# A two-block transformer on one Trainium2 core: new order in the opening and around two projections, other products in retention

## The chip, the cores and the metric

The kernel runs on one core of one Trainium2 (trn2) chip. The metric is device time in microseconds of one execution; lower is better. The core's engines are TensorE (PE; its weight loads are PEld), VectorE (DVE), ScalarE (ACT), GpSimd (POOL) and SyncE (SP), which issues the DMAs. [...]

## The reference

The input `x` is 256 tokens of width 1024, in float32. Two blocks follow one another.

The first block: `h = rms_norm(x)`, a projection `h @ w_in` gives q, k, v of four attention branches (stick-breaking, dilated, forgetting, differential) and a gate; `x += sum(sigmoid(gate) * (branch @ w_branch)) @ w_out`; then `x += square(relu(rms_norm(x) @ w_up)) @ w_down`, and a last `rms_norm(x)`.

The second block has a retention layer and a sparse-attention layer, each followed by a SwiGLU layer, all with a norm in front and behind. In retention q and k are rotated in pairs, the scores are multiplied by a decay, the outputs are normed per head, multiplied by `silu(g)` and projected back with `w_ro`:

```
q, k = rotate_pairs(q, cos, sin), rotate_pairs(k, cos, sin) / 16
o = (q @ k.T * decay) @ v                      # four heads, v is 512 wide
o = o * rsqrt(mean(o * o) + eps) * silu(g)
x = x + rms_norm(o @ w_out)
```

The sparse-attention layer projects shared keys and values and queries, and a small gate matrix (`w_ng`, 48 columns), and projects back with `w_no`.

## The kernel before, in words

Tokens lie in two row tiles (t = 0, 1) of 128. All large products are done at near float32 accuracy from two parts: every operand is split into a high part `hi` (fp32r) and a low part `lo = x - hi`, and three products hi·hi, hi·lo, lo·hi are summed (`mm3`, L246 to L251). A weight comes in halves of 128 x 1024 (or 128 x 772 for the first): `each_half` (L225) issues the DMA into one of four `raw` buffers, ScalarE makes `whi` (L234), VectorE `wlo` (L237); six such pairs can be held (`wsp`), more where a pool is added. This is called a split below.

`Inputs.a(t)` norms the rows t: two square sums (ScalarE L406, VectorE L411), their mean (L414), the power -0.5 on GpSimd (L416), the scaling `xn` (L193, L194). `Inputs.b(t)` transposes `xn` on TensorE (L436) and makes the eight column pairs of hi (ScalarE L209) and lo (VectorE L210).

`an_groups` (L297) starts each layer: two groups of four weight halves. All halves that can be held are multiplied for one row tile first; ahead of the last of them stands `inp.b(1)`, so the second rows' norm is needed only there; then the second row tile follows. `project_back` (L357) ends each layer: the products of all chunks but the last three go into four banks (two row tiles, two halves of the columns) at once; the last six halves are held and used row tile by row tile: for t = 0 all held halves into bank 0 and then all into bank 1, `residual(0)` and `nxt.a(0)` follow, then t = 1, where `nxt.b(0)` stands before the last half.

Two forms of a projection with the weight as the stationary operand: `ws_chunk` (L343) does three products of 256 columns per 128 rows of the weight, `ws_wide` (L259) one of 512 columns (hi and lo of x side by side, L274) and one of 256 (L276), and adds the two halves of the bank on ScalarE (L277) and VectorE (L278).

In the opening (L499 to L505) SyncE issues the first rows, two small constants, the second rows and then weights. TensorE does 12 products of zeros (`warm_up`). `run` writes `inp.a(0)`, the second rows' DMA, `inp.b(0)`, `inp.a(1)` in this order, then `mix`.

The mlp's `residual` (L1065) adds the rows (L449), norms them, applies the final gain (L1070), and is followed by the norm for retention. In retention, `rotated` (L1124) multiplies the projection's bank with cosine and sine (L1127, L1129) and adds on GpSimd (L1130); `scores` uses the result in full float32; `outputs` (L1158) multiplies the weights `at` with v in full float32 (L1164, L1166). In `nsa` the small matrix `wng` is split before the layer's `an_groups`.

The order of the instructions on each engine is set when the program is built. A planner of the framework takes them from the order of the code, and places one earlier when it expects its inputs earlier; engines run their lists in that order. `tc.issue_after(i)` adds an edge: what is written inside it is placed behind `i` on `i`'s engine. `behind(engine)` (L471) does so with the engine's last instruction so far.

## Time and profile before

| | |
|---|---|
| median of the runs shown (1204.67 to 1211.26) | 1204.8 us |
| the profiled execution | 1208.24 us |
| its span, first to last instruction | 1206.5 us |
| TensorE busy, share of the span | 98% |
| VectorE, ScalarE, GpSimd | 67%, 55%, 7% |
| HBM, over the span | 173 GB/s |

All rows come from the one profiled execution. Times in a view are microseconds from the span's start. In a timeline row stand start, duration, engine, line, operation, output<-inputs, shape, and in brackets the idle time of the engine before it with what ended it. [...]

### The profile page before, as it was taken

How to read it: one execution, taken by the hardware profiler on the slowest of the kernel's cores; microseconds unless marked ns; L12 is line 12 of the kernel's file. 1: busy time of each engine (PE TensorE's matmuls, PEld its weight loads, DVE VectorE, ACT ScalarE, POOL GpSimd, SP SyncE). 2: the span in 40 equal slices, each digit the busy share in tenths (PEclk: the TensorE clock that was granted, in tenths of full speed). 3: DMA queues.
4: the chain of work that ended last, by engine and by line, in shares of the span. 5: the costliest groups of instructions: out<-in, count | busy, mean ns of one | idle time of the engine just before them, and what ended most of it. 6: DMA issues, size and time to landing. Idle time of an engine off the chain costs nothing.

```text
span 1206.5 us, 18129 instructions
## 1 busy us (share of the span) xinstructions
PE 1184.8 (98%) x6848; PEld 1014.4 (84%) x6848; DVE 806.3 (67%) x1413; ACT 662.9 (55%) x1148; POOL 80.8 (7%) x87
## 2 busy tenths in 40 slices
PE   8999999999999998999999999999999999999997
PEld 6999889887888887899878888888889877888886
DVE  7757877667746667557456665657778967655663
ACT  5545765655644454543555554556567876645561
POOL 1000001200000000012000000000100530000000
PEclk8999999999999999999999999999999999999999
DMA  7654454536455565554546355556655226555560
GB/s 239 196 175 158 140 191 158 175 126 230 161 192 187 191 208 181 177 194 158 166 148 213 120 192 189 192 185 212 209 194 179 72 70 205 179 189 186 189 205 35
DMA packets 60775, 210.11 MB, mean 174 GB/s; under 512 B 7120, under 2 KB 9808, under 8 KB 60560
## 3 DMA queue, kind: packets, MB, share of 16 engines
q1 hardware_dynamic: 60688, 208.95, 53.0%
q8 instruction: 54, 0.88, 0.3%
q14 instruction: 33, 0.27, 0.1%
HBM read 207.84 MB, written 1.08 MB: 173 GB/s over the span
## 4 chain that ended last, share of the span: by engine, by line
PE 82%; DVE 7%; DMA 5%; ACT 3%; issue 1%; POOL 0%; SPq 0%; DVEq 0%; POOLq 0%; ACTq 0%
PE b L274 19%; PE b L249 15%; PE b L251 15%; PE b L250 15%; PE b L276 9%; DVE wlo L237 3%; ACT whi L234 1%; PE b L436 1%; DMA raw<-w_up 1%; DMA raw<-w_no 1%; DMA raw<-w_rv 1%; PE b L1536 1%; DMA raw<-w_ck 1%; DMA wng<-w_ng 1%; ACT s L1503 1%
## 5 line engine op out<-in xcount | busy, mean ns | idle before, releaser
L237 DVE TENSOR_TENSOR wlo<-raw,whi 128x1024 fp32r<-128x1024 f32 (+3 forms) x432 | 470.9, 1103 | 265.1 <-ACT whi L234 262.2
L234 ACT ACTIVATE whi<-raw 128x1024 fp32r<-128x1024 f32 (+1 forms) x384 | 401.6, 1050 | 383.6 <-issue 116.5
L274 PE MATMUL b<-x,whi 128*128 128x512 f32 x1024 | 362.7, 398 | 0.0
L276 PE MATMUL b<-x,wlo 128*128 128x256 f32 x1024 | 286.3, 280 | 0.0
L249 PE MATMUL b<-whi,x 128*128 128x512 f32 (+1 forms) x720 | 283.9, 395 | 1.8 <-ACT x L209 1.0
L250 PE MATMUL b<-wlo,x 128*128 128x512 f32 (+1 forms) x720 | 280.7, 390 | 1.0 <-DVE wlo L237 0.8
L251 PE MATMUL b<-whi,x 128*128 128x512 f32 (+1 forms) x720 | 279.8, 390 | 0.6 <-DVE x L210 0.6
L274 PEld LDWEIGHTS b<-x,whi 128*128 128x128 f32 x1024 | 192.2, 188 | 45.9 <-issue 0.3
L276 PEld LDWEIGHTS b<-x,wlo 128*128 128x128 f32 x1024 | 193.1, 189 | 0.9
L249 PEld LDWEIGHTS b<-whi,x 128*128 128x128 f32 x720 | 136.1, 189 | 34.5 <-ACT x L209 4.3
L251 PEld LDWEIGHTS b<-whi,x 128*128 128x128 f32 x720 | 136.3, 189 | 29.9 <-DVE x L210 1.3
L250 PEld LDWEIGHTS b<-wlo,x 128*128 128x128 f32 x720 | 136.4, 189 | 28.7 <-DVE wlo L237 1.9
L249 PE MATMUL b<-x,whi 128*128 128x256 f32 x480 | 137.6, 287 | 0.0
L251 PE MATMUL b<-x,wlo 128*128 128x256 f32 x480 | 135.5, 282 | 0.4 <-DVE wlo L237 0.4
L250 PE MATMUL b<-x,whi 128*128 128x256 f32 x480 | 135.4, 282 | 0.0
L249 PEld LDWEIGHTS b<-x,whi 128*128 128x128 f32 x480 | 91.5, 191 | 2.1 <-issue 1.5
L251 PEld LDWEIGHTS b<-x,wlo 128*128 128x128 f32 x480 | 91.5, 191 | 0.6 <-DVE wlo L237 0.6
L250 PEld LDWEIGHTS b<-x,whi 128*128 128x128 f32 x480 | 91.6, 191 | 0.1
L416 POOL TENSOR_TENSOR rstd<-ms,mhalf 128x1 f32<-128x1 f32 x22 | 13.8, 626 | 686.5 <-DVE ms L414 686.5
L210 DVE SCALAR_TENSOR_TENSOR x<-b,gc,x 128x128 fp32r<-128x128 f32 x112 | 36.7, 348 | 20.2 <-ACT x L209 18.3
L209 ACT ACTIVATE x<-b,gc 128x128 fp32r<-128x128 f32 x112 | 37.9, 367 | 21.7 <-PE b L436 16.5
L1503 ACT ACTIVATE s<-s,nm 128x128 f32<-128x128 f32 (+1 forms) x64 | 28.2, 444 | 2.6 <-DVE rz L1507 1.4
(277 smaller groups left out, 1014.8 us busy)
## 6 DMA issues: line engine op xcount, KB each, us to landing
raw<-w_fi SPq DMA_DIRECT2D x88, 512.0 KB, 4.5
raw<-w_fo SPq DMA_DIRECT2D x44, 512.0 KB, 4.5
raw<-w_gate SPq DMA_DIRECT2D x32, 512.0 KB, 4.2
raw<-w_up SPq DMA_DIRECT2D x32, 512.0 KB, 3.9
raw<-w_down SPq DMA_DIRECT2D x32, 512.0 KB, 3.9
raw<-w_qk SPq DMA_DIRECT2D x24, 512.0 KB, 4.1
raw<-w_rv SPq DMA_DIRECT2D x16, 512.0 KB, 4.8
raw<-w_rqk SPq DMA_DIRECT2D x16, 512.0 KB, 4.5
```

What stands on the lines that cost most here:

```text
L209: k.nc.scalar.activation(hi, ps[:, j, :], AF.Copy, scale=g)
L210: k.nc.vector.scalar_tensor_tensor(lo, ps[:, j, :], g, hi.bitcast(F32), op0=OP.mult, op1=OP.subtract)
L234: nc.scalar.activation(hi[:, :n], r, AF.Copy)
L237: nc.vector.tensor_tensor(lo[:, c], r[:, c], hi[:, c].bitcast(F32), op=OP.subtract)
L249: mm(out, lhs[0], rhs[0], start=start, stop=False)
L250: mm(out, lhs[0], rhs[1], start=False, stop=False)
L251: mm(out, lhs[1], rhs[0], start=False, stop=stop)
L274: mm(ps.rearrange("p a t -> p (a t)"), half[0][:, s], x[2][:, k].rearrange("p a t -> p (a t)"), start=k == 0, stop=False)
L276: mm(ps[:, 0], half[1][:, s], x[0][:, k, :], start=False, stop=k == KT - 1)
L416: nc.gpsimd.tensor_tensor(r, ms, self.mhalf[:, :1], op=OP.pow)
L436: self.nc.tensor.transpose(ps[:, j, :], src[:, j * 128:(j + 1) * 128], self.ident)
L1503: nc.scalar.activation(s[:, a, i, :], s[:, a, i, :], AF.Exp, bias=nm[:, a, i:i + 1], scale=-1.0, accum_out=z[:, a, i:i + 1])
```

## The change

Seven edits:

- Opening: the second rows' DMA goes behind the DMAs of two weight halves; the splits are queued behind the first rows' scaling (`rows_done`), the second rows' norm behind the first rows' column pairs (`columns_done`).
- Two sets of 12 products that nobody reads (`keep_warm`, 256 columns, bf16), behind the first rows' transposes and behind the first half's products.
- The GpSimd biases of the differential branch are queued behind the second rows' norm.
- `project_back`, where it has four chunks (w_out, w_no): for t = 0 the held halves go into bank 0 and bank 1 alternately, one half apart. In the others the order stays.
- Entry of retention: the splits of w_rv from the third half on are queued behind the add of the first rows' residual in the mlp.
- Retention: q and k use `ws_wide`, and the scores of a head come one chunk later; the outputs use `mm3` on split operands instead of float32 products.
- Sparse attention: the split of `wng` is written and queued behind the layer's first products.

```
-    def an_groups(self, groups, n, inp, order=(0, 1), extra=0):
+    def an_groups(self, groups, n, inp, order=(0, 1), extra=0, then=None):
...
                 for j in range(4):
+                    queued = self.queued(self.rows_done if len(hs) > 1 or then else ())
...
-                    hs.append((i, 2 * j, next(chunk)))
+                    with queued:
+                        hs.append((i, 2 * j, next(chunk)))
+                    if then and len(hs) == 2:
+                        then()
...
                 mul(j, order[0])
+                if then and j == 0:
+                    self.keep_warm()
...
         accs = [[self.bank() for _ in range(2)] for _ in range(2)]
+        self.rows_done = ()
...
+            lead = min(len(held), 1 if nk == KT else len(held))
             for t in range(2):
-                for banks in ((0,), (1,)) if t == 0 or not nxt else ((0, 1),):
-                    for a in held[:-1]:
-                        self.as_t(accs[t], *a, t, banks)
-                    if t and nxt:
+                if t == 0 or not nxt:
+                    order = [(i, 0) for i in range(lead)]
+                    for i in range(len(held)):
+                        order += [(i + lead, 0)] * (i + lead < len(held)) + [(i, 1)]
+                else:
+                    order = [(i, n) for i in range(len(held)) for n in range(2)]
+                for i, n in order:
+                    if t and nxt and (i, n) == (len(held) - 1, 0):
                         nxt.b(0)
-                    self.as_t(accs[t], *held[-1], t, banks)
+                    self.as_t(accs[t], *held[i], t, (n,))
...
+    def keep_warm(self):
+        w = self.ident.bitcast(BF)
+        ps = self.bank()[:, :256]
+        with self.behind(self.nc.tensor):
+            for _ in range(WARM):
+                self.nc.tensor.matmul(ps, w[:, :128], w, start=True, stop=True)
+    def lasts(self):
+        order = list(reversed(self.nc.cur_bb.bb.instructions))
+        return [next(i for i in order if i.engine == e.engine) for e in (self.nc.scalar, self.nc.vector)]
+    def queued(self, instructions):
+        es = ExitStack()
+        for i in instructions:
+            es.enter_context(self.tc.issue_after(i))
+        return es
...
             inp.a(0)
-            nc.sync.dma_start(self.x[:, 1, :], self.I["x"][:, 1, :])
+            self.rows_done = self.lasts()
             inp.b(0)
-            inp.a(1)
+            self.keep_warm()
+            columns_done = self.lasts()
+            def second_rows():
+                nc.sync.dma_start(self.x[:, 1, :], self.I["x"][:, 1, :])
+                with self.queued(columns_done):
+                    inp.a(1)
+                self.second_norm = [i for i in nc.cur_bb.bb.instructions if i.engine == nc.gpsimd.engine][-1:]
...
-                nc.gpsimd.tensor_scalar(b, mk[:, kind, :], -slope, None, op0=OP.mult)
+                with self.queued(self.second_norm):
+                    nc.gpsimd.tensor_scalar(b, mk[:, kind, :], -slope, None, op0=OP.mult)
...
-            vs = self.an_groups([("w_v", 0), ("w_v", 1)], NB, inp)
+            vs = self.an_groups([("w_v", 0), ("w_v", 1)], NB, inp, then=second_rows)
...
             def residual(t, acc):
                 self.add_residual(t, acc)
+                if t == 0:
+                    self.rows_done = self.lasts()
...
-            def rotated(s, ps):
-                a = tp.tile([128, 2, T], F32, tag=f"rot{s}", name="rot")
+            def rotated(s, i):
+                a = self.ws_wide("w_rqk", i, xin, tp.tile([128, 2, T], F32, tag=f"rot{s}", name="rot"))
                 b = tp.tile([128, 2, T], F32, tag="rotb", name="rotb")
-                nc.vector.tensor_tensor(a, ps, cs, op=OP.mult)
                 for j in range(2):
-                    nc.vector.tensor_tensor(b[:, j, :], ps[:, 1 - j, :], sn[:, j, :], op=OP.mult)
+                    nc.vector.tensor_tensor(b[:, j, :], a[:, 1 - j, :], sn[:, j, :], op=OP.mult)
+                nc.vector.tensor_tensor(a, a, cs, op=OP.mult)
                 nc.gpsimd.tensor_tensor(a, a, b, op=OP.add)
...
-                    if s == 0 and qk:
+                    if s == 1 and qk:
                         scores(h - 1, *qk)
...
+                    steps += 1
+                    if steps == 2 and g == 0:
+                        scores(3, *qk)
+                    if steps == (3 if g == 0 else 1):
+                        src = [v[:, t, g * 512:(g + 1) * 512] for t in range(2)] + [at[:, g, :]]
+                        for tag, x in zip(("rot0", "rot1", "rotb"), src):
+                            hl = [tp.tile([128, 2, T], F32, tag=tag, name=tag).rearrange("p a t -> p (a t)").bitcast(F32R)
+                                  [:, :x.shape[1]] for _ in range(2)]
+                            self.split(*hl, x)
+                            parts.append(hl)
...
-                    mm(p, at[:, g, t * 128:t * 128 + 128], v[:, 0, vs], start=True, stop=t == 0)
+                    self.mm3(p, [x[:, t * 128:t * 128 + 128] for x in w], v0, True, t == 0)
                     if t:
-                        mm(p, at[:, g, T:384], v[:, 1, vs], start=False, stop=True)
+                        self.mm3(p, [x[:, T:384] for x in w], v1, False, True)
...
-            wg = tp.tile([128, KT, 96], F32R, name="wg")
-            self.split(wg[:, :, :48], wg[:, :, 48:], raw.rearrange("p (k c) -> p k c", k=KT))
...
                 nc.scalar.activation(vn[:, t, :], ps[1][t], AF.Copy)
+            wg = tp.tile([128, KT, 96], F32R, name="wg")
+            with self.queued(self.lasts()):
+                self.split(wg[:, :, :48], wg[:, :, 48:], raw.rearrange("p (k c) -> p k c", k=KT))
```

## Rows read from the trace of the kernel before

**Rows 1.** The page's busy times and its line of granted clock, 40 slices.
```profile
PE 1184.8 (98%) x6848; PEld 1014.4 (84%) x6848; DVE 806.3 (67%) x1413; ACT 662.9 (55%) x1148; POOL 80.8 (7%) x87
...
PEclk8999999999999999999999999999999999999999
```

**Rows 2.** Timeline of the opening: start, duration, instruction, idle time before it.
```profile
5.83 0.54 POOL L416 TENSOR_TENSOR rstd<-ms,mhalf 128x1 f32<-128x1 f32 x1 [4.75 <-DVE ms L414]
9.13 0.69 DVE L411 CUSTOM_DVE_ANT_0 junk<-res 128x512 bf16<-128x512 f32 x1 [3.44 <-DMA res<-x]
...
10.12 0.85 ACT L234 ACTIVATE whi<-raw 128x772 fp32r<-128x772 f32 x1 [0.18 <-DMA raw<-w_v]
...
10.63 2.12 PE L436 MATMUL b<-cm,xn 128*128 128x128 f32 x8 [4.55 <-DVE xn L193]
...
11.79 0.37 ACT L209 ACTIVATE x<-b,gc 128x128 fp32r<-128x128 f32 x1 [0.20 <-PE b L436]
...
21.11 0.42 PE L249 MATMUL b<-whi,x 128*128 128x386 f32 x1
```

**Rows 3.** Stretches: from:to, length, busy per engine, granted clock, DMA share, GB/s.
```profile
10.60:15.70 5.10, 5.07 (x17) 3.94 (x17) 3.82 (x11) 4.87 (x12) 0.38 (x1) 0.50 0.51 161
...
476.60:480.00 3.40, 2.72 (x11) 2.56 (x12) 1.17 (x4) 1.71 (x4) 0.02 (x1) 0.50 0.00 0
...
998.80:1002.20 3.40, 3.40 (x9) 2.62 (x9) 2.26 (x3) 1.49 (x2) 0.00 (x0) 0.50 0.81 252
...
543.00:555.80 12.80, 12.80 (x106) 12.70 (x105) 8.74 (x11) 4.24 (x4) 3.50 (x2) 1.00 0.50 164
```

**Rows 4.** Timeline of TensorE at the ends of w_out and w_no.
```profile
277.78 0.74 PE L249 MATMUL b<-whi,mx 128*128 128x512 f32 x2 [0.75 <-ACT whi L234]
...
995.80 0.47 PE L249 MATMUL b<-whi,x 128*128 128x512 f32 x1
997.04 0.50 PE L250 MATMUL b<-wlo,x 128*128 128x512 f32 x1 [0.76 <-DVE wlo L237]
...
998.56 1.03 PE L249 MATMUL b<-whi,x 128*128 128x512 f32 x2 [0.79 <-ACT whi L234]
```

**Rows 5.** Timeline at the entry of retention.
```profile
469.98 1.29 DVE L237 TENSOR_TENSOR wlo<-raw,whi 128x512 fp32r<-128x512 f32 x2 [2.81 <-ACT whi L234]
...
471.19 0.68 DVE L449 TENSOR_TENSOR res<-res,b 128x512 f32<-128x512 f32 x1
...
477.28 1.94 PE L436 MATMUL b<-cm,xn 128*128 128x128 f32 x8 [3.34 <-DVE xn L193]
```

**Rows 6.** Timeline of TensorE: L249 in w_rqk, 30 apart, and L274 in w_up, 34 apart.
```profile
544.65 0.28 PE L249 MATMUL b<-x,whi 128*128 128x256 f32 x1
...
555.45 0.28 PE L249 MATMUL b<-x,whi 128*128 128x256 f32 x1
...
440.34 0.40 PE L274 MATMUL b<-x,whi 128*128 128x512 f32 x1
...
452.35 0.40 PE L274 MATMUL b<-x,whi 128*128 128x512 f32 x1
```

**Rows 7.** Chain that ended last, around a retention output: start, us, what.
```profile
586.53 0.23 PE b L251
...
588.07 1.72 PE b L1164 x4
```

**Rows 8.** Groups of VectorE instructions: count, busy us, mean ns, idle before.
```profile
L237 DVE TENSOR_TENSOR wlo<-raw,whi 128x1024 fp32r<-128x1024 f32 x328 | 402.6, 1233 | 243.9 <-ACT whi L234 241.1 <-PE b L251 0.6 <-issue 0.4
...
L278 DVE TENSOR_TENSOR up<-b,up 128x256 f32<-128x256 f32 x36 | 15.1, 421 | 15.5 <-ACT up L277 15.5
...
L243 DVE TENSOR_TENSOR x<-sg,x 128x512 fp32r<-128x512 f32 x18 | 12.3, 685 | 0.7 <-ACT x L242 0.7
```

**Rows 9.** Timeline at the entry of sparse attention.
```profile
877.60 0.52 ACT L242 ACTIVATE wg<-wng 128x384 fp32r<-128x384 f32 x1 [0.78 <-DMA wng<-w_ng]
...
878.69 0.50 PE L249 MATMUL b<-whi,x 128*128 128x512 f32 x1 [0.48 <-ACT x L209]
```

**Rows 10.** Timeline of VectorE in the rotation, beside a GpSimd add from 544.62.
```profile
544.97 2.02 DVE L237 TENSOR_TENSOR wlo<-raw,whi 128x1024 fp32r<-128x1024 f32 x1
```

More of the change, by code (lines that the diff above doesn't have):

```diff
@@ L489, in run @@
             self.ps = self.pool(es, "ps", 8, bass.MemoryType.PSUM)
+            self.rows_done = ()
             nc.scalar.preload_act_table_set("natural_log_exp_and_others")
@@ L502, in run @@
             inp.a(0)
-            nc.sync.dma_start(self.x[:, 1, :], self.I["x"][:, 1, :])
+            self.rows_done = self.lasts()
             inp.b(0)
-            inp.a(1)
+            self.keep_warm()
[5 more added lines that the diff above has]
+                self.second_norm = [i for i in nc.cur_bb.bb.instructions if i.engine == nc.gpsimd.engine][-1:]
             with ExitStack() as e1:
                 qkp = self.pool(e1, "b1qk", 5)
-                mx = self.mix(inp, cm, qkp)
+                mx = self.mix(inp, cm, qkp, second_rows)
                 inp = Inputs(self, ("mlp_norm_g",))
@@ L517, in run, with mix @@
             self.ffn(inp, 1, None)
-    def mix(self, inp, cm, qkp):
+    def mix(self, inp, cm, qkp, second_rows):
         nc, I = self.nc, self.I
@@ L1144, in retention @@
                 for s in range(2):
-                    rot.append(rotated(s, self.ws_chunk("w_rqk", 2 * h + s, xin)))
-                    if s == 0 and qk:
+                    rot.append(rotated(s, 2 * h + s))
+                    if s == 1 and qk:
                         scores(h - 1, *qk)
@@ L1152, in gates, with outputs @@
                 sg = tp.tile([128, 2, 512], F32, tag="sg", name="sg", bufs=1)
+                parts, steps = [], 0
                 for _ in self.an_steps("w_rg", g, 512, xin,
                                        lambda t, ps: nc.scalar.activation(sg[:, t, :], ps, AF.Silu)):
-                    pass
-                return sg
-            def outputs(g, sg):
-                vs = slice(g * 512, (g + 1) * 512)
+                    steps += 1
[8 more added lines that the diff above has]
+                            parts.append(hl)
+                return sg, parts
+            def outputs(g, sg, parts):
+                v0, v1, w = parts
                 ss = self.st.tile([128, 2], F32, tag="ss2", name="ss2")
@@ L1186, in retention @@
                 sg = gates(g)
-                if g == 0:
-                    scores(3, *qk)
-                else:
+                if g:
                     transposed(yn)
-                yn = outputs(g, sg)
+                yn = outputs(g, *sg)
             e1.close()
```

## Prediction

> **What bounds the kernel now.** The page's first part comes first: TensorE is busy for 1184.8 of 1206.5 us, VectorE for 806.3, ScalarE for 662.9 [rows 1]. So TensorE sets the end, and there are two things to look for: products that could be cheaper, and the few places where it waits. The granted-clock line of the page shows the second kind: every slice is at 9 but the first, at 8. I then read the timeline where TensorE's rows show idle time, and the stretches of half clock. Four places matter.
>
> The opening. The norm factor of the first 128 rows leaves GpSimd at 5.83+0.54 us, but VectorE's next instruction is the square sum of the second rows, which waits 3.44 us for their DMA and starts at 9.13; only then comes the first rows' scaling, and with it TensorE's first transposes (10.63, after 4.55 us without a product) [rows 2]. [...]
>
> The two 8-row projections (w_out, w_no), where TensorE waits for the last weight halves [rows 4]; the entry of retention, where it waits 3.34 us for the normalised rows and then works at 0.50 [rows 3, 5]; and a small wait in the sparse-attention entry.
>
> Against what the numbers hold: the span is 1206.5, the execution 1208.24, 1.7 around it; the median of the runs shown is 1204.8. I take terms from the trace and subtract them from the median. A difference of 1%, 12 us, is about what a measurement of this kernel can tell from no change.
>
> **The change part by part.**
>
> *Opening.* The second rows' DMA goes behind two weight halves, their norm behind the first rows' eight column pairs, and every weight split behind the first rows' scaling. So the scaling can follow GpSimd at 6.4 us, and the transposes start half a microsecond behind it, near 7.0 instead of 10.63: 3.6 us earlier. The half clock of 10.6 to 15.7 costs 5.1 × 0.5 = 2.55 us [rows 3]; with warm-up products until 6.08 (10.63 less the idle 4.55), transposes from 7.0 and 12 filler products behind them, TensorE is hardly idle, so I expect the clock to stay up. Together 6.15 us at most. What is late next: the weight splits. TensorE runs six halves for the first rows before it needs the second rows; before, the product behind the second rows' transposes starts at 21.11 [rows 2]. Until then ScalarE must do eight column copies of 0.37, six splits of 0.85 and one norm of about 1.5, in all 9.6 us, and VectorE about as much; from 7.0 that ends near 17 to 18, not at 15. So I take 3.0 of the 6.15. The two sets of filler products are 24 × 256 columns; 256 columns take 0.12 us at full clock (a third of a triple [rows 6]), so 2.9 us, beside waits for weights; if that cover is gone they cost 2.9. The second rows' norm is the added wait: queued behind it on ScalarE and VectorE are the later splits, and TensorE's transposes of the second rows wait for it; its scaling ends some 4 us behind the eighth column, near 15, needed at 17. The GpSimd biases behind it are products of the mask for a branch that comes much later: nothing. SyncE's queue issues the second rows' DMA two places later, and the two weights one place earlier. Bounds: -2 (fillers bare, second rows late by a little) to 6.
>
> *w_out and w_no.* For the first rows, the held halves are now used for bank 0 and bank 1 alternately, so a half that is late is wanted later. The number of products is the same. w_out: a wait of 0.75 for the last half [rows 4]; a bank is three products of 0.23 us [rows 7], and four banks more pass before that half is wanted, 2.8 us, against 0.75: gone, 0.9 with the restart. w_no: waits of 0.76 and 0.79, which with the start-up of the products around them are 2.0 us, and the clock at 0.50 from 998.8 to 1002.2, worth 1.7 [rows 3, 4]. The last half's high part lets its product go at 998.56, its low part, one VectorE split of 1.23 later [rows 8], comes near 999.8. The old order would have asked for that half at 996.5 (the bank before it begins at 995.80), the new one asks four banks later, at 999.3, so 0.5 remains: 2.0 + 1.7 - 0.5 = 3.2. The norm of the first rows starts that much earlier, its chain is as long as before. Bounds: 0 to 4.6 for both; I take 0.9 and 3.2.
>
> *Entry of retention.* The w_rv splits from the third half on are queued behind the first rows' residual. Before, VectorE waits 2.81 us for the seventh half's split, does it at 469.98, and only then adds the residual (471.19), whose bank had been ready near 467 (30 products of 0.23 before the last one at 473.9) [rows 5, 7]. Two norms follow, and TensorE gets its transposes at 477.28, 3.34 us late. Without that wait the chain starts 4 us earlier and the transposes are ready when TensorE arrives. Lost there: the 3.34 us, and half of the 2.7 us from 477.28 to 480.0 in which the clock is 0.50: 4.7 in all [rows 3, 5]. What is late next: VectorE. Splits of halves three to seven (5 × 1.29) used to run before 471, in gaps; now they run between 467 and 485, with two norm chains (an estimate of 4.0 each, five passes over 512 columns at 0.69 [rows 8] and small ones), eight column copies of 0.35 and 1.4 for the second residual: from 473.3 about 13.7 us for the 12 us to the need of the seventh half. So 1.5 comes back as waiting: 3.2. The four weight buffers behind the waiting splits stay full meanwhile, so SyncE's queue stands; the halves it would fetch are wanted after 485 only. Bounds: -4 (all five splits, 6.5 us, ahead of the first chain, and the clock falls again) to 4.7.
>
> *Rotation of q and k.* Eight chunks go from three products of 256 columns to one of 512 and one of 256. Three take (555.45 - 544.65) / 30 = 0.360 us, the pair (452.35 - 440.34) / 34 = 0.353 [rows 6]; 8 × 16 × 0.0068 = 0.9 us. [...] Each chunk adds two ScalarE copies and two VectorE adds of 0.42 [rows 8], and the scores of a head now come one chunk later. VectorE is busy for 8.74 us of a 12.8 us stretch of two chunks [rows 3]; 1.7 more still fits: hidden.
>
> *Retention outputs.* Six full-precision passes per head, 0.43 us each (1.72 for four [rows 7]), become nine of 0.23: 2.58 - 2.07 = 0.51, four heads 2.05 us. For that, three splits per head: ScalarE 1.7, VectorE 1.9 us (0.69 for 512 columns [rows 8]) beside the 11 us of a gate projection. Hidden; bare it would cost 4 × 1.9 = 7.7.
>
> *Sparse-attention entry.* ScalarE waits for a small weight's DMA until 877.60, and the column copy queued behind that split holds TensorE for 0.48 [rows 9]; the split moves behind the projections, where the first use is 17 us away: 0.5.
>
> **Sum.** 3.0 (opening) + 0.9 + 3.2 (w_out, w_no) + 3.2 (retention entry) + 0.9 + 2.05 (rotation, outputs) + 0.5 = 13.75 us. 1204.8 - 13.75 = 1191.05; for the profiled execution it would be 1194.5.
>
> **The rivals.**
>
> *Handed back (1197).* The openings of both kinds are bound by splits: TensorE arrives earlier and waits for VectorE. For it: at both places I found VectorE's work within 10% of the time there is. Then opening and retention entry give 2 together instead of 6.2, and the clock falls once more in one of them (1.7): 13.75 - 4.2 - 1.7 = 7.85. Against it: both begin with a wait that has nothing to do with load.
>
> *Both entries pay in full (1187).* If the splits fit into the gaps and the clock never falls, the opening gives 6 and the retention entry 4.7: 18.25 us. For it: VectorE and ScalarE are at 67% and 55% over the span [rows 1]; against it the work counted above for these places.
>
> *VectorE becomes the bound in retention (1212, slower).* Place: rotation and gates. Price: the added VectorE work all on the path, 8 × 0.84 + 4 × 1.9 = 14.4 us; GpSimd's eight adds at up to 0.8 each, 6.4. A VectorE split beside a GpSimd add took 2.02 us where such a split takes 1.23 on average [rows 8, 10]. Then 1204.8 - 13.75 + 20.8 = 1212; if each of the eight waits also brings a stretch at 0.50 (1.7 each, as in w_no), 1225. It decides at the point where VectorE needs more than TensorE's 12.4 us for two chunks; from 8.74 + 1.7 = 10.4 it lacks 2. [...]
>
> *The ordering edges do nothing (1198).* If the planner's order was not what made VectorE wait, only w_out, w_no, rotation and outputs pay: 7.05. Against it: the rows show the instruction that waits, and what stands behind it.
>
> **How the numbers follow.** Forecast 0.50 (1186 to 1195, its middle below the 1% line at 1192.8); handed back 0.22; both in full 0.13; edges do nothing 0.08; VectorE bound 0.07. Faster by over 1%: 0.13 + 0.38 of the forecast's half + 0.02 = 0.53. Slower by over 1% needs the last rival with the clock: 0.05. Within 1%: 0.42. The range, 1184 to 1200, holds the forecast, the first rival and most of the second and fourth.
>
> **What would show it.** Right: first transposes near 7 us and no stretch at 0.50 after 6 us; the product behind the second rows' transposes near 18; L449 of the first rows before the third w_rv split, and no TensorE gap over 1 us in front of the transposes; no wait over 0.6 us in w_out and w_no, no half clock at w_no; outputs as rows of 0.23. Wrong: half clock in the opening all the same; a gap of over 2 us at the entry of retention, filled on VectorE by splits; TensorE rows in the rotation that wait for VectorE; fillers with a weight's products ready behind them.

## The result, and the profile after

| | before | after |
|---|---|---|
| median (runs) | 1206.07 us (4) | 1196.4 us (4) |
| lowest to highest | 1204.67 to 1211.26 | 1194.91 to 1197.22 |
| ratio, 95% interval | | 0.9917 [0.9898, 0.9936] |
| profiled execution, its span | 1208.24, 1206.5 | 1197.22, 1195.4 |

The kernel is 0.83% faster, 9.7 us between the medians and 11.0 between the profiled executions, inside the range 1184 to 1200; I had forecast 13.75. (The 1204.8 from which I subtracted was the median of the first three of the four runs before; with the fourth it is 1206.07.)

Where it came from is read from TensorE's rows: I take the start of the same instruction in both traces at seven marks, and the differences of the stretches add up to that of the spans (the start of a layer is its "entry", which ends at the transposes of the second rows). The numbers in brackets are the marks, before and after.

| TensorE's stretch | before | after | gain | forecast |
|---|---|---|---|---|
| opening: start to the product behind the second rows' transposes | 21.11 | 19.76 | 1.35 | 3.0 |
| to the mlp's first transposes (288.92, 286.94) | 267.81 | 267.18 | 0.63 | 0.9, with the next |
| to the mlp's second transposes (302.45, 299.90) | 13.53 | 12.96 | 0.57 | |
| entry of retention (489.03, 483.16) | 186.58 | 183.26 | 3.32 | 3.2 |
| to the next layer's entry (689.38, 680.83): rotation, outputs | 200.35 | 197.67 | 2.68 | 2.95 |
| to the first transposes behind w_no (1011.86, 1000.68) | 322.48 | 319.85 | 2.63 | 3.7 |
| to the end | 194.60 | 194.74 | -0.14 | 0 |
| sum | 1206.46 | 1195.42 | 11.04 | 13.75 |

Two terms were too large, the opening and w_no. The sum of 11.0 is that of two executions; by the medians it is 9.7, and the experiment with the kernel before, below, shows where one execution of it differs from another. The page after, busy times and granted clock (the share of TensorE's full clock that the profile shows as granted; half clock stands for a stretch at 0.50):

```profile
PE 1179.6 (99%) x6756; PEld 1008.0 (84%) x6756; DVE 819.0 (69%) x1441; ACT 672.6 (56%) x1176; POOL 83.0 (7%) x87
...
PEclk9999999999999999999999999999999999999999
```

The 8 of the first slice is gone [rows 1]. Stretches of the kernel after (from:to, length, busy per engine, granted clock, DMA share, GB/s): where TensorE had 0.50 [rows 3] it has 1.00, and VectorE is nearly full at the places of the change (6.83 of 7.44 us, 3.39 of 3.40, 7.91 of 8.40).

```profile
10.60:15.70 5.10, 4.48 (x27) 3.34 (x27) 4.51 (x14) 4.01 (x9) 0.27 (x1) 1.00 0.95 313
12.29:19.73 7.44, 6.45 (x33) 4.69 (x32) 6.83 (x17) 4.52 (x10) 3.44 (x3) 1.00 0.74 212
473.20:476.60 3.40, 3.34 (x19) 2.74 (x19) 3.39 (x8) 2.82 (x9) 0.00 (x0) 1.00 0.74 210
992.20:1000.60 8.40, 7.18 (x32) 5.61 (x30) 7.91 (x18) 6.54 (x12) 1.46 (x2) 1.00 0.69 231
543.00:555.80 12.80, 12.80 (x75) 11.17 (x74) 10.63 (x16) 5.52 (x9) 3.76 (x3) 1.00 0.51 168
```

Timeline of the opening after ("x8" joins eight instructions to one row):

```profile
7.05 1.09 PE L450 MATMUL b<-cm,xn 128*128 128x128 f32 x8 [1.56 <-DVE xn L193]
...
8.82 0.56 DVE L237 TENSOR_TENSOR wlo<-raw,whi 128x386 fp32r<-128x386 f32 x1 [1.82 <-ACT whi L234]
...
11.15 0.85 ACT L234 ACTIVATE whi<-raw 128x772 fp32r<-128x772 f32 x1 [0.60 <-DMA raw<-w_v]
...
16.27 0.49 DVE L193 TENSOR_SCALAR xn<-res,rstd 128x512 f32<-128x512 f32 x1 [0.44 <-POOL rstd L430]
...
16.31 2.72 POOL L670 TENSOR_SCALAR bias<-mk 128x384 f32<-128x384 bf16 x2
...
16.67 3.06 DVE L237 TENSOR_TENSOR wlo<-raw,whi 128x386 fp32r<-128x386 f32 x5
...
19.76 0.42 PE L249 MATMUL b<-whi,x 128*128 128x386 f32 x1
```

The first transposes start at 7.05 as forecast; but VectorE gets its first split at 8.82, ScalarE waits for the third half until 11.15, and five splits beside two biases take 3.06 us and end at 19.73, when TensorE goes on [rows 2]. Of 3.6 us gained at the start 1.35 are left.

Entry of retention after:

```profile
464.56 0.69 DVE L463 TENSOR_TENSOR res<-res,b 128x512 f32<-128x512 f32 x1 [3.43 <-PE b L251]
...
473.26 1.06 PE L450 MATMUL b<-cm,xn 128*128 128x128 f32 x8 [0.95 <-DVE xn L193]
```

The mark at its end, before and after:

```profile
489.03 1.03 PE L436 MATMUL b<-cm,xn 128*128 128x128 f32 x8
```

```profile
483.16 1.09 PE L450 MATMUL b<-cm,xn 128*128 128x128 f32 x8
```

w_no after:

```profile
990.45 0.50 PE L250 MATMUL b<-wlo,x 128*128 128x512 f32 x1 [0.43 <-DVE wlo L237]
...
1000.68 1.09 PE L450 MATMUL b<-cm,xn 128*128 128x128 f32 x8 [1.30 <-DVE xn L193]
```

In retention the add follows its bank at once, and the wait falls from 3.34 to 0.95 [rows 5]. In w_no the waits have moved. A matmul's pace is read from the starts: from 984.86 to 989.63 after, the record of one lasts 0.39 to 0.40 us and the next starts 0.23 behind. With that 0.23 taken off between starts, the waits were, before, 1.01 + 0.95 for weight halves [rows 4], after 0.59 for one and 1.46 for the norm of the first rows.

### The profile page after: what moved, and what is told of

Its sections match the earlier page's. It is cut to its first block, busy times and chain, and to the rows that moved or that the text cites. A ratio compares the mean times of both kernels' runs of the same rounds, so it can differ in the third digit from the quotient of the medians.

```text
span 1195.4 us, 18025 instructions
## 1 busy us (share of the span) xinstructions
PE 1179.6 (99%) x6756; PEld 1008.0 (84%) x6756; DVE 819.0 (69%) x1441; ACT 672.6 (56%) x1176; POOL 83.0 (7%) x87
## 4 chain that ended last, share of the span: by engine, by line
PE 87%; DVE 6%; ACT 3%; DMA 2%; issue 1%; POOL 0%; SPq 0%; DVEq 0%; POOLq 0%; ACTq 0%
PE b L274 22%; PE b L249 16%; PE b L251 15%; PE b L250 15%; PE b L276 11%; DVE wlo L237 2%; PE b L450 1%; ACT whi L234 1%; PE b L1592 1%; DMA raw<-w_v 1%; DMA raw<-w_fi 1%; ACT s L1559 1%; PE b L1575 1%; DMA raw<-w_up 1%; PE b L690 0%
## 5 line engine op out<-in xcount | busy, mean ns | idle before, releaser
L274 PE MATMUL b<-x,whi 128*128 128x512 f32 x1152 | 408.2, 398 | 0.0
L249 PE MATMUL b<-whi,x 128*128 128x512 f32 (+1 forms) x720 | 281.0, 391 | 1.2 <-ACT x L209 1.2
L274 PEld LDWEIGHTS b<-x,whi 128*128 128x128 f32 x1152 | 216.3, 188 | 51.8 <-issue 0.3
L249 PEld LDWEIGHTS b<-whi,x 128*128 128x128 f32 x720 | 135.4, 188 | 32.4 <-ACT x L209 4.4
L249 PE MATMUL b<-x,whi 128*128 128x256 f32 x352 | 101.2, 287 | 0.0
L250 PE MATMUL b<-x,whi 128*128 128x256 f32 x352 | 99.2, 282 | 0.0
L249 PEld LDWEIGHTS b<-x,whi 128*128 128x128 f32 x352 | 67.0, 190 | 2.1 <-issue 1.5
L250 PEld LDWEIGHTS b<-x,whi 128*128 128x128 f32 x352 | 67.0, 190 | 0.1
```

What stands on the lines that cost most here:

```text
L249: mm(out, lhs[0], rhs[0], start=start, stop=False)
L250: mm(out, lhs[0], rhs[1], start=False, stop=False)
L274: mm(ps.rearrange("p a t -> p (a t)"), half[0][:, s], x[2][:, k].rearrange("p a t -> p (a t)"), start=k == 0, stop=False)
```

## The experiments

Most variants below were run once; they are read from stretches of their traces, since one time of one kernel moves by a microsecond or two (1194.91 to 1197.22 in the four of the kernel after). "The changed kernel" is the kernel after, "the mark" of the opening the product behind the second rows' transposes. How well a stretch repeats: the opening's mark came at 19.11 to 19.86 in eight traces of kernels with the same opening; the entry of retention took 183.26 to 183.28 in nine of ten traces that share it (183.65 in the tenth); the stretch from the second transposes of sparse attention to the first behind w_no 133.46 to 134.50 in six (136.88 before). The kernel before has its profile and, behind the opening, a second trace, told below. No run takes back the new order of products in `project_back`, `ws_wide`, the output products or the split of `wng` alone: their shares are read from their stretches.

**Without the unread products.**

```
-                if then and j == 0:
-                    self.keep_warm()
...
-            self.keep_warm()
```

> The changed kernel without its two sets of 12 unread products; the rest as it is. Read from the trace: the granted clock of the opening, and the start of the product behind the second rows' transposes (19.76 us with them, 21.11 before the change). If the unread products keep the clock up and it matters, a stretch at 0.50 shows behind 8 us, and that product starts at 21 or later. If TensorE waits for the splits whatever its clock is (my theory: VectorE, which ends the sixth half at 19.73, sets the end of the opening), a stretch at 0.50 may show, but that product starts within 0.3 us of 19.76. If the fillers stand in the way of ready products, it starts 0.3 us or more earlier.

Measured, stretches of this kernel:

```profile
11.30:15.00 3.70, 3.40 (x10) 2.97 (x11) 3.25 (x10) 3.02 (x8) 0.28 (x1) 0.50 1.01 353
15.00:19.80 4.80, 4.80 (x23) 4.63 (x22) 4.04 (x8) 1.76 (x4) 3.16 (x3) 0.68 0.64 180
```

The clock fell to 0.50 from 11.3 us, and stayed there for some 3 us of the second stretch, an estimate from its mean of 0.68 as 0.50 first and 1.00 then; the mark came at 19.85, the upper edge of what the same opening shows with them. By my price (half of the length) that clock would have cost over 3 us. It cost 0 to 0.7, as if TensorE at 0.50 still kept up with the splits. In one of eleven traces with the unread products (that of the edge behind the whole norm, below) the clock was at 0.50 as well, behind a wait of 1.95 us, and the mark came at 19.30:

```profile
7.66:11.07 3.41, 3.41 (x19) 2.73 (x18) 2.14 (x6) 2.92 (x7) 0.00 (x0) 0.50 1.02 389
```

So the clock stayed up in ten of eleven traces with the unread products and fell in the one without; in this order of work it was not on the path (marks of 19.85 and 19.30 with the fall, 19.11 to 19.86 in the eight traces with the same opening).

**Biases later.**

```
+            late = self.st.tile([128, 1], F32, tag="late", name="late")
+            nc.gpsimd.tensor_tensor(late, v[:, 1, :1], self.mhalf[:, :1], op=OP.add)
+            self.second_norm = [i for i in nc.cur_bb.bb.instructions if i.engine == nc.gpsimd.engine][-1:]
```

> The changed kernel with the GpSimd biases of the differential branch behind one small GpSimd add that reads v of the second rows, so that they run near 28 us and not at 16.3 to 19.0. If the biases hold up VectorE's splits (two of them took 0.86 us beside a bias, 0.55 alone), the splits of 16.7 to 19.7 take 0.55 each, and the product behind the second rows' transposes starts 0.5 to 0.9 us before 19.76. If weights' arrival or ScalarE set that end, the splits are shorter but the product starts within 0.1 us of 19.76. The time as a whole moves by less than 1 us either way, which a single time does not show.

Measured, timeline:

```profile
16.35 2.44 DVE L237 TENSOR_TENSOR wlo<-raw,whi 128x386 fp32r<-128x386 f32 x5
```

```profile
18.90 0.42 PE L249 MATMUL b<-whi,x 128*128 128x386 f32 x1
```

The same five splits take 2.44 instead of 3.06. The mark is 0.86 earlier than in the changed kernel's profile, 0.2 earlier than the earliest of the other traces. A second kernel with late biases, among the timed ones below, has its mark at 19.15, inside what the others show. So the biases lengthen the splits beside them by 0.6 us; that the opening as a whole loses 0.2 to 0.9 by them rests on one trace and is not shown. I had put them at nothing, "for a branch that comes much later": true of who needs them, but not of whom they run beside.

**The second rows' norm behind four halves.**

```
-                    if then and len(hs) == 2:
-                        then()
+                    if then and len(hs) in (2, 4):
+                        then[len(hs) // 4]()
...
-                mx = self.mix(inp, cm, qkp, second_rows)
+                mx = self.mix(inp, cm, qkp, (second_load, second_rows))
```

> The changed kernel with the second rows' norm written behind the fourth weight half of the opening and not behind the second (their DMA stays). VectorE then splits the fourth half before it takes the square sum; its queue waited 0.45 us for the norm factor ahead of the scaling, and the split of the fourth half, whose high part was ready at 13.25, ended at 17.53. If VectorE's amount of work sets the end of the opening (my theory), the sum is the same and the product behind the second rows' transposes starts within 0.4 us of 19.76 (less 0.4 if the wait of 0.45 goes). If the early norm is what holds up the weights, that product starts a microsecond or more earlier, near 18.5; if the second rows are what is late, it starts a microsecond later.

Measured: the second rows' transposes start at 18.37 in one piece instead of between 16.81 and 20.00, and the product behind them (there another product) at 19.22: more than the 0.4 us that I allowed ahead of the profile's 19.76, but within what the unchanged order shows. The mlp's first transposes, which are the same product in both, come at 286.53, between the 286.28 and 287.03 of the unchanged order. VectorE is busy for 6.54 of the 7.27 us up to the end of its last split (19.56, with the other order 19.73). Another order of the same work, the same end: that fits my theory that VectorE's amount sets it.

**The kernel before, kept warm.**

```
-        for _ in range(WARM):
+        for _ in range(WARM + 18):
```

> The kernel before, with 30 instead of 12 products of zeros at the start, so that TensorE works until about 10 us and the 4.55 us without a product ahead of the first transposes are filled; nothing else. I had put the half clock of 10.6 to 15.7 at 2.55 us on the path. If that price was right, the product behind the second rows' transposes starts near 18.6 and not at 21.11. If the splits set the end of the opening at either clock (my theory now), there is no stretch at 0.50, and that product starts within 0.4 us of 21.11.

Measured, stretches:

```profile
10.60:15.70 5.10, 3.26 (x14) 1.80 (x14) 4.40 (x12) 5.10 (x12) 0.48 (x1) 1.00 0.59 153
15.90:19.70 3.80, 3.80 (x15) 3.40 (x16) 3.52 (x10) 2.56 (x6) 0.00 (x0) 0.55 0.98 349
```

Neither number came: the product started at 22.56. The planner put splits ahead of the second rows' scaling, so the order changed with the warm-up, and the clock fell later. The price of the half clock alone can't be taken from this run; only that a clock of 1.00 from 10.6 to 15.7 did not by itself bring the product nearer (22.56 against 21.11).

The run shows something that I had not asked for. From 34 us on every engine has the same order of instructions as in the kernel before, so that it is a second trace of it there. TensorE waits at the entry of retention and at w_no as before, for 2.45 us instead of 3.34 and for 0.27 and 0.56 instead of 0.76 and 0.79; but behind these waits the granted clock stays at 1.00, where the profile before has 0.50 [rows 3]:

```profile
477.31 1.06 PE L436 MATMUL b<-cm,xn 128*128 128x128 f32 x8 [2.45 <-DVE xn L193]
```

```profile
476.60:480.00 3.40, 2.69 (x16) 2.42 (x17) 2.03 (x5) 2.52 (x6) 0.04 (x1) 1.00 0.00 0
998.00:1002.00 4.00, 4.00 (x19) 3.10 (x18) 3.46 (x7) 3.56 (x5) 0.00 (x0) 1.00 0.89 324
```

The entry of retention takes 184.44 us here instead of 186.58. From a product of the attention (980.00 before, 970.43 after) to the first transposes behind w_no are 29.66 us instead of 31.86, where six traces with the changed kernel's order of w_no take 30.04 to 30.25. So against this trace the entry of retention gains 1.2 us and not 3.3, and w_no nothing: by 2.1 and 2.2 us the gain there differs between the two traces of the kernel before, of which one shows 0.50 behind these waits and the other 1.00. Over the eleven timed executions before, the mean granted clock was 0.994 to 0.997; the profile has 0.993, this trace 0.997, the changed kernel again 0.998 to 0.999.

**Retention without its edge.**

```
-                if t == 0:
-                    self.rows_done = self.lasts()
```

> The changed kernel without the edge at the entry of retention (the w_rv splits wait for nothing). If the edge is what gained there, the shift of 3.3 us against the kernel before goes away: TensorE's wait ahead of the first rows' transposes is 3 us or more again, the clock falls to 0.50 behind it, and the second rows' transposes come 3 to 3.7 us after 483.16. If the order would have come out so anyway (the rival that the edges do nothing), they stay within 0.3 us of 483.16.

Measured, timeline, and a stretch:

```profile
473.71 1.94 PE L450 MATMUL b<-cm,xn 128*128 128x128 f32 x8 [2.97 <-DVE xn L193]
```

```profile
472.70:477.20 4.50, 3.49 (x13) 3.14 (x14) 1.68 (x5) 2.34 (x6) 0.34 (x1) 0.50 0.00 0
```

Wait and half clock are back, and the entry takes 187.69 us instead of 183.26: the edge is worth 4.4 in this trace, more than the 3.3 between before and after. How much of it is the clock, which fell at this place in one of the two traces of the kernel before, one trace does not tell. The rival that the edges do nothing falls.

**w_no with an edge behind the whole norm of the first rows.** In `project_back`, behind `nxt.a(t)`:

```
+                if t == 0 and name == "w_no":
+                    self.rows_done = self.lasts()
```

> The changed kernel with one more edge: the splits of the last layer's first weight, from the third half on, behind the norm of w_no's first rows. In the changed kernel TensorE waits 1.46 us (pace taken off) ahead of the first rows' transposes at 1000.68; the chain from the end of bank 1 to them takes 8.1 us where it took 6.6 before the change, with seven half splits of 0.69 in VectorE's queue and a ScalarE split of 1.05 ahead of the square sum. If those splits lengthen the chain (my theory), the chain takes 6.6 again, the wait falls to 0.2 or less, and the second rows' transposes of that layer (1013.28) come 1.0 to 1.4 us earlier. If the waits only move, the same time comes back as waits for low parts right behind, and the second rows' transposes stay within 0.3 us.

Measured, timeline:

```profile
998.65 1.03 PE L452 MATMUL b<-cm,xn 128*128 128x128 f32 x8
...
1001.87 0.50 PE L249 MATMUL b<-whi,x 128*128 128x512 f32 x1 [0.79 <-ACT x L209]
...
1007.98 1.06 ACT L234 ACTIVATE whi<-raw 128x1024 fp32r<-128x1024 f32 x1 [1.34 <-DMA raw<-w_fi]
```

Both were right in half: from the end of bank 1 (992.01) to the transposes the chain takes 6.64 us again, without a wait; but the next layer's second transposes come 15.2 us later instead of 12.6, as the splits from the third half on now stand behind the norm, and the weights that want their buffers behind them. 1.6 gained against the profile (0.8 to 1.8 against the six traces), 2.6 lost.

**w_no with the edge behind the residual, and on ScalarE alone.** Both ahead of `nxt.a(t)`; the second with `self.lasts()[:1]`:

```
+                if t == 0 and name == "w_no":
+                    self.rows_done = self.lasts()
```

> The same edge as at the entry of retention, for w_no: the splits from the third half on behind the first rows' residual (square sums, gain and add) on both engines, and not behind the norm that follows. The chain to the first rows' transposes should lie between the changed kernel (8.1 us from the end of bank 1) and the run with the edge behind the whole norm (6.1 from the square sum of bank 1), so 0.8 to 1.4 us earlier; behind it the stretch to the second rows' transposes (12.6 us) grows by 0 to 2.6. My theory, VectorE and the weights' arrival have little room there: the sum of both is between -0.8 and +1.0. The rival, that the entry of retention carries over: the sum is -1 or better.

> The changed kernel with one more edge: the splits of the last layer's first weight, from the third half on, behind ScalarE's square sum of bank 1 of w_no's first rows, on ScalarE alone. In the changed kernel that square sum starts 1.2 us behind the end of bank 1, since a split of 1.05 (its weight half lands at 992.5) stands ahead of it. My theory: it is ScalarE's place in the queue that counts; then the time from the layer before (transposes at 866.42) to the first rows' transposes, 134.26 us, shrinks by 0.5 to 1.2, and the time from there to the second rows' transposes stays at 12.6, so that the second rows' transposes gain too. Rival, as in the run with the edge behind the whole norm, where 1.6 us were gained ahead of the transposes and 2.6 lost behind them: the later splits are late, and the stretch of 12.6 grows by as much as the first shrinks.

Measured: behind the residual the stretch takes 132.40 us and the next one 12.45 (changed kernel 134.26 and 12.60); on ScalarE alone 131.62 and 12.60. So the rival of the first and the theory of the second, though with more than its 0.5 to 1.2: nothing came back. The two can't be told apart: on every engine their instructions came out in the same order, so that one is a repeat of the other, and whether the edge on VectorE does anything is open. The second seemed to be worth 2.6 us, so it was timed.

**The timed runs.** The changed kernel again; the edge on ScalarE; with it the late biases; with it retention's edge moved behind the norm and gain of the mlp's residual:

> The changed kernel itself once more, as the measure for the three beside it. Its opening is read again: in four runs whose opening is the same, the product behind the second rows' transposes started at 19.11 to 19.30 us, in the changed kernel's own profile at 19.76. I expect 19.1 to 19.8 here, so that what one look shows of the opening holds to about 0.3 us, and a time of 1195 to 1198.

> The changed kernel with the edge at w_no on ScalarE alone (the splits of the last layer's first weight from the third half on stand behind the square sum of bank 1). In one look it took 2.6 us off the stretch ahead of the first rows' transposes, and gave nothing back behind them. If that holds, the time is 2 to 3 us under the changed kernel's of the same rounds, 1193 to 1195; if the look fell on a good execution, within 1 us of it.

> The same, and the GpSimd biases behind the copy of v. The run with late biases alone started the product behind the second rows' transposes at 18.90 us, 0.2 to 0.4 before the runs with the same opening, and the gain was no longer seen ahead of retention. So 0 to 0.4 us under the kernel with the edge alone; theory and rival (that later waits take the opening's gain back) cannot be told apart by the whole time, only by the opening and the w_out stretch in the trace.

> The kernel with the edge at w_no on ScalarE, and the edge at the entry of retention moved from behind the add of the first rows' residual to behind its norm and gain (as the edge at w_no that took 2.0 us there). In the changed kernel TensorE still waits 1.11 us ahead of the first rows' transposes of retention, with four half splits between the add and the scaling. If splits in the chain make that wait, it falls to 0.3 or less, and the second rows' transposes come 0.5 to 1.1 us earlier. If VectorE has no room (twice two norms in 20 us), the wait moves behind the transposes, and the stretch from the mlp's second rows' transposes to retention's (183.26 us in four runs) stays or grows by up to 1.5.

| | median (runs) | ratio to before (1205.63), interval |
|---|---|---|
| changed again | 1196.27 (6) | 0.9926 [0.9911, 0.9940] |
| edge on ScalarE at w_no | 1195.88 (5) | 0.9918 [0.9902, 0.9934] |
| and late biases | 1195.28 (6) | 0.9918 [0.9903, 0.9932] |
| and retention's edge moved | 1198.57 (6) | 0.9945 [0.9931, 0.9959] |

The changed kernel repeats (its opening's mark at 19.39). The edge on ScalarE does not hold what its first trace promised: 0.4 us of medians, not to be told from none. Timelines of w_no, changed again, and with the edge:

```profile
998.56 1.09 PE L450 MATMUL b<-cm,xn 128*128 128x128 f32 x8 [1.90 <-DVE xn L193]
```

```profile
990.87 0.58 ACT L422 ACTIVATE junk<-b 128x512 bf16<-128x512 f32 x1
...
991.43 0.59 ACT L424 ACTIVATE junk<-b 128x512 bf16<-128x512 f32 x1
...
998.66 1.09 PE L452 MATMUL b<-cm,xn 128*128 128x128 f32 x8 [0.98 <-DVE xn L193]
```

With the edge the square sum of bank 1 follows the bank at once, and TensorE waits 0.98 instead of 1.90; the stretch takes 132.90 instead of 133.46. The 131.62 was a good execution. Yet in all five traces with such an edge w_no is shorter than in the six without: 28.26 to 29.34 us from the product of the attention to the first transposes, against 30.04 to 30.25, and the stretch behind them is no longer (12.44 to 12.60, against 12.56 to 12.60 and once 13.47). The gain of about a microsecond is there in the traces, and too small for the whole times. Late biases have the opening's mark at 19.15 and the entry of the mlp at 13.36 instead of 12.99; without late biases that entry took up to 13.34, so neither a gain nor its loss behind the opening can be seen. Retention's moved edge loses:

```profile
472.47 1.06 PE L452 MATMUL b<-cm,xn 128*128 128x128 f32 x8 [0.60 <-DVE xn L193]
...
479.30 0.51 PE L249 MATMUL b<-whi,x 128*128 128x512 f32 x1 [1.26 <-ACT x L209]
...
485.99 1.09 PE L452 MATMUL b<-cm,xn 128*128 128x128 f32 x8 [0.96 <-DVE xn L193]
```

0.35 less waiting ahead of the first transposes, and two new waits of about a microsecond behind them; the entry takes 185.62 instead of 183.26, which is beyond the 1.5 that I had allowed. By whole times no version measurably beats the changed kernel.

## Why the prediction was right, and where its terms were off

*What bounds.* Right: TensorE is busy for 99%, and what was gained is its idle or half-clocked time and cheaper products. The chances leaned the wrong way, with 0.53 for over 1%: 0.83% was measured. Nor is a difference of 12 us as much as a measurement of this kernel needs: the interval of the ratio, 0.9898 to 0.9936, is 4.6 us wide. All sizes below are against one profile of the kernel before.

*Opening, 3.0, measured 1.35 in the profile, 1.25 to 2.0 in the repeats.* The step that failed is "the half clock of 10.6 to 15.7 costs 2.55 us" together with "from 7.0 that ends near 17 to 18". The first counted a clock as lost time where TensorE was waiting for splits anyway: without the unread products the clock fell to 0.50, and the mark stayed within the repeats (19.85, in 19.11 to 19.86). That is shown for the new order; for the old one the run that kept it warm leaves it open. The second let VectorE's work run from 7.0 without gaps; it could not begin before the first half's high part was there (8.82), stood idle for 1.0 us behind that (0.42 behind 11.87, where the third half had come late, 0.17, and 0.44 for the second norm), and had 0.6 us more to do beside the biases. From 8.82 my own estimate of 9.6 us would have given 18.4, and with these two 20.1; it came to 19.73. The fillers were right: without them the mark came no earlier.

*w_out, 0.9, measured 0.63, and 0.57 behind it.* The mechanism was right; the wait for the last half shrank (0.75 [rows 4] to 0.34) but did not vanish. That the halves that came earlier also shortened the mlp's entry, which I had not counted, is not shown: it took 12.74 to 13.34 in the traces without late biases, 13.12 in the second trace of the old one.

*w_no, 3.2.* With sparse attention 2.63 of 3.7; the latter's part is 0.77 (forecast 0.5): a product went from 884.95 to 875.63, 9.32, where the entry stood at 8.55. Another 0.25 came between there and w_no, where nothing was changed; from the product of the attention on the gain was 1.6 (31.86 to 30.25 us), about the 1.7 for the clock, and nothing against the trace before in which the clock did not fall (29.66). The step that failed is "its chain is as long as before". From the end of bank 1 to the first transposes it took 6.64 us before (1005.22 to 1011.86) and takes 8.11 (992.57 to 1000.68), since alternating banks end together. ScalarE's square sum of bank 1 before:

```profile
1005.25 0.60 ACT L408 ACTIVATE junk<-b 128x512 bf16<-128x512 f32 x1 [0.90 <-PE b L251]
```

And after, of both banks, with a split between them:

```profile
992.28 0.58 ACT L420 ACTIVATE junk<-b 128x512 bf16<-128x512 f32 x1
...
992.85 1.05 ACT L234 ACTIVATE whi<-raw 128x1024 fp32r<-128x1024 f32 x1
993.80 0.59 ACT L422 ACTIVATE junk<-b 128x512 bf16<-128x512 f32 x1
```

Bank 0's square sum used to begin at 1001.77, 3.5 us ahead of the end of bank 1; now it begins at 992.28, 0.3 ahead, and that of bank 1 at 993.80, 1.23 behind the bank, since a ScalarE split of the next layer (992.85) stands ahead of it. From that square sum on the chain takes 6.88 us, before 6.61. So the 2.0 us of waiting moved to the transposes, instead of falling to 0.5, and "no wait over 0.6 us" was wrong there. The runs with an edge shortened the stretch (131.6 to 132.9 us, without one 133.5 to 134.5), and the one with the whole norm ahead of the splits showed what limits that: the products right behind the norm want these splits.

*Entry of retention, 3.2, measured 3.32.* Right in mechanism: the add behind its bank, a shorter wait, no half clock; without the edge 4.4 are lost. The share given back showed as 0.95 ahead of the transposes. Its size had not followed from my working: the terms listed there add up to 18.65 us for the 18 from 467 to 485, not to 13.7 for 12. That the sum came so near owes something to the profile before, in which the clock fell: against the other trace it is 1.2.

*Rotation and outputs, 2.95, measured 2.68.* Right: from the first product of w_rqk to the first output 0.8 (525.71 and 587.91 before, 519.91 and 581.29 after), to the start of w_ro 1.95. By the rows' paces, 0.360 and 0.353 us, I had 0.9 for the first. A head's outputs are nine rows of 0.23 (581.29 to 583.34), the splits hidden, and no TensorE row there waits for VectorE, busy for 10.63 of 12.80 us; I had said 10.4.

*The rivals.* Handed back (1197) was named for the openings of both kinds: it held in the opening, and in w_no, for which it was not named, but not in retention, and the time lies nearer to it than to 1191. Both lie inside the range, so that the time alone does not tell them apart; the stretches do. That both entries pay in full, that the edges do nothing, and that VectorE binds in retention, fell.

## What to carry to other kernels

Before a stretch at half clock, or a wait, is given a price, count the work of the engines that feed TensorE from the arrival of their first data, and see whether it still ends later: here 3.7 us at 0.50 in the opening, without the unread products, left the mark at 19.85, within the repeats. And a clock that fell in one execution need not fall in the next (from 476.6 on 0.50 in the profile before, 1.00 in the trace kept warm): a profile of the kernel before that shows the fall can promise more than another trace of it does, here 3.3 us and 1.2 at the entry of retention. The wait that another order of products removed came back here where those products had covered a chain, a norm (at w_no 0.95 for the last half before, 1.46 for the norm after); write down what ran beside the old order. One trace of each kernel shows what an engine waits for; a gain of 2 us in a stretch still has to be repeated, before as well as after: the edge at w_no took 2.6 us off its stretch in the first pair of traces and 0.6 in the second.

## What the runs showed of the hardware

The same program order and nearly the same wait ended once with half clock and once without. Ahead of w_no's first transposes TensorE sat idle for 1.87 us in the kernel with the second norm behind four halves, and the clock was at 0.50 from 1000.87 on; in the changed kernel again it sat idle for 1.90 us, and the clock stayed at 1.00. The stretch to the second transposes took 13.47 and 12.58 us, so 3.41 us at half clock cost 0.9 there, and not half of their length:

```profile
1000.87:1004.28 3.41, 3.41 (x11) 2.74 (x10) 3.10 (x9) 2.22 (x7) 0.00 (x0) 0.50 0.80 250
```

The same pair of products (512 and 256 columns) ran at two steady paces, 0.347 and 0.353 us. In the kernel after, two stretches of thirty pairs in one layer:

```profile
717.61 0.40 PE L274 MATMUL b<-x,whi 128*128 128x512 f32 x1
...
728.01 0.39 PE L274 MATMUL b<-x,whi 128*128 128x512 f32 x1
...
734.27 0.39 PE L274 MATMUL b<-x,whi 128*128 128x512 f32 x1
...
744.87 0.40 PE L274 MATMUL b<-x,whi 128*128 128x512 f32 x1
```

10.40 / 30 = 0.347 us, then 10.60 / 30 = 0.353, at the same granted clock. In the changed kernel's second trace the same two stretches read:

```profile
716.95 0.40 PE L274 MATMUL b<-x,whi 128*128 128x512 f32 x1
...
727.35 0.39 PE L274 MATMUL b<-x,whi 128*128 128x512 f32 x1
...
733.62 0.40 PE L274 MATMUL b<-x,whi 128*128 128x512 f32 x1
...
744.02 0.39 PE L274 MATMUL b<-x,whi 128*128 128x512 f32 x1
```

Both at 0.347. Over any ten pairs the pace was 0.346 to 0.347 in these three stretches and 0.352 to 0.355 in the one at 0.353: so the second stretch of one program ran at 0.353 in one execution and at 0.347 in another. From the last transposes to the end the kernel took 182.1 to 183.3 us with the same instructions there, so that 1.2 us of a whole time is decided behind all that was changed. Why there are two paces, no run here tells.

In places GpSimd and VectorE took longer beside each other: the power of a norm took 0.54 us alone (5.94) and 0.93 in the entry of retention (467.27), where VectorE had a split at the same time; two splits took 0.86 beside a bias (16.67, 17.92), one alone 0.55 (9.81); and the bias that ran beside the first of them took 1.47, where the median of the four is 1.17. Neither stood still for the other's whole instruction there: the split ran from 16.67 to 17.53 inside the bias, which ran from 16.31 to 17.78.
